# Two half-height matmul streams in the MLP of a small decoder trunk

## The chip, the cores and the metric

One core of one Trainium2 chip runs the whole program in one launch. The metric is device time in microseconds (us) of one execution. The engines have names that the profile uses: TensorE is PE (its weight loads are a row of their own, PEld), VectorE is DVE, ScalarE is ACT, GpSimd is POOL, SyncE is SP (it issues most DMAs). SBUF is the on-chip working memory of 128 partitions; PSUM is the accumulator memory that TensorE writes, eight banks of 512 fp32 values per partition.

## The reference, cut to what matters

A decoder trunk of two layers, 256 tokens, width 1024. Layer 0 has a mixer of convolution and pooling, layer 1 an attention mixer; each layer ends with a gated MLP of inner width 2816, and a final norm follows. The MLP is what the change touches:

```python
def conv_ffn(h, w_in, conv_w, conv_b, w_out):
    z = h @ w_in
    u, g = z[..., :D_FF], z[..., D_FF:]
    a = causal_dwconv(u, conv_w) + conv_b      # width 3 along the tokens
    return (jax.nn.silu(a) * g) @ w_out

h = h + conv_ffn(rmsnorm(h, ffn_norm_g[layer]), ...)
```

All values are fp32. The kernel keeps nearly that precision on TensorE by splitting each operand in two parts of a shorter format, hi and lo, and adding three products: hi by hi, hi by lo, lo by hi.

## The kernel before, in words

**Tiling.** Activations lie transposed, features on the 128 partitions and the 256 tokens along the row. The inner width of the MLP is cut into 22 chunks of 128 (index f). A step f computes the two input products of its chunk, u and g; each contracts 1024 features in eight chunks k of 128 rows. For each k, `in_halves` (lines 298 to 302) issues two matmuls. The first has the hi part of the weight as stationary operand and the hi and lo parts of the activation as one moving operand of 512 columns; it fills both halves of an accumulator bank. The second has the lo part of the weight and the hi part of the activation, 256 columns, and adds to the second half. That is 8 x 2 x 2 = 32 matmuls a step. The accumulators are `zu` and `zg`, one bank each, taken in turn from a pool of four banks, so that two steps are in flight.

**Behind the products.** `added` (line 527) adds the two halves of a bank: ScalarE copies one (line 532), VectorE adds the other (line 533). `gate` (line 536) scales by the norm's row, does the convolution (lines 388, 391, 392), SiLU (line 542) and the product with g (line 544), and splits the result y into hi and lo (lines 310 and 316).

**Output products.** y of chunk f is used LAG = 4 steps later. In layer 0 `Acc.add` (line 328) maps it to the eight chunks of 128 output features, three matmuls of 256 columns each (`mm3`, lines 276 to 279), 24 in all, on four accumulator banks `acc` that are kept through the layer. In layer 1 `TokenAcc.add` (line 350) has y as stationary operand and the weights as moving one, so that tokens end up on the partitions: four groups of three matmuls of 512 columns, 12 in all, on four banks `ta`, which first get the residual by 16 transposes (line 347).

**Order.** TensorE's order is that of the code (`manual_schedule(engines=ORDERED)`, line 54): u of step f, then g, then the output products of chunk f - 4, through the list `ffn_steps` (lines 66 to 71). After the last input step come the output products of chunks 18 and 19, and the last two chunks are closed chunk by chunk with what follows the MLP. The other engines' orders are made by a planner from the program and its own costs of each instruction.

**Weights.** They stream from HBM in blocks of 128 x 1024 fp32 (512 KB): u, g and output block of each step. SP loads a block into one of eight staging buffers (line 141), ScalarE makes the hi part (line 133), VectorE the lo part (line 134); hi and lo lie in a ring of seven pairs, and a pair is free again when the last matmul that reads it is done. Blocks are emitted in order of use, up to six ahead of the last one used (`ahead`, line 154).

**Elsewhere.** The attention's last product (`mix`, lines 745 to 752) writes the two heads of a pair to the two halves of the partitions of one bank; its stationary operand has 64 columns, so that each head uses one half of the array's columns. The norm's statistics use one-column matmuls (line 225). The MLP of layer 0 also writes a table for the attention to HBM by a DMA of POOL (line 595).

Of the kernel before, what the change touches and what calls it, by code (L numbers as in the profile page):

```python
# [18 lines left out]
P = 128  # L19
T = 256  # L20
D = 1024
NK = D // P
DFF = 2816
NF = DFF // P
# [9 lines left out]
LAG = 4  # L34
# [16 lines left out]
def trunk(ctx, tc, a, out):  # L51
    nc = tc.nc
# [83 lines left out]
    def emit_block(i):  # L136
        key, src = blocks[i]
        st, hi, lo = block_tiles(i)
        piece = 512 if i < 2 else BLK
        for s in range(0, BLK, piece):  # L140
            nc.sync.dma_start(st[:, s:s + piece], src[:, s:s + piece])
            cut(st, hi, lo, s, s + piece)
        done[key] = (hi, lo)
# [10 lines left out]
    def ahead(n=LOOK):  # L154
        while state["next"] < min(state["used"] + 1 + n, len(blocks)):
            emit_block(state["next"])
            state["next"] += 1

    def weights(key):
        state["used"] = max(state["used"], place[key])  # L160
        ahead(0)
        return done.pop(key)
# [18 lines left out]
    def col(i):  # L181
        return vec[:, i:i + 1]

    def new_hg():

        t = hgp.tile([P, NK, 2, T], F32R, tag="hg", name="hg")
        return t[:, :, 0, :], t[:, :, 1, :], t
# [12 lines left out]
    hg = new_hg()  # L200
# [46 lines left out]
    first = fst.tile([P, NK, FIRST], F32, name="first")  # L247
# [50 lines left out]
    def in_halves(z, w, k, x, first=False, last=False):  # L298

        wh, wl = (t[:, k * P:(k + 1) * P] for t in w)  # L300
        nc.tensor.matmul(z, wh, x[:, k], start=first, stop=False, skip_group_check=True)  # L301
        nc.tensor.matmul(z[:, 1, :], wl, x[:, k, 0, :], start=False, stop=last, skip_group_check=True)  # L302

    def split(pool_, src, scale, name, bufs=None, between=None):

        kw = {} if bufs is None else {"bufs": bufs}
        hi = pool_.tile([P, T], F32R, tag=name + "h", name=name + "h", **kw)
        lo = pool_.tile([P, T], F32R, tag=name + "l", name=name + "l", **kw)
        if scale is None:
            nc.scalar.copy(hi, src)  # L310
        else:
            nc.scalar.activation(hi, src, AF.Copy, scale=scale)
        if between is not None:
            between()
        if scale is None:
            nc.vector.tensor_sub(lo, src, hi.bitcast(F32))
        else:
            nc.vector.scalar_tensor_tensor(lo, src, scale, hi.bitcast(F32), op0=ALU.mult, op1=ALU.subtract)
        return hi, lo

    class Acc:
# [13 lines left out]
        def add_all(self, w, y):  # L335
            for dc in range(NK):
                self.add(dc, w, y, False)

    class TokenAcc:


# [13 lines left out]
        def add_all(self, w, y):  # L355
            for i in range(2):
                for n in range(2):
                    self.add(i, n, w, y, False)

    def close(acc, tail, b, between=None):  # L360

        for dc in (2 * b, 2 * b + 1):
            if dc % 2 and between is not None:
                between()
            for i, (w, y) in enumerate(tail):
                acc.add(dc, w, y, i == len(tail) - 1)
        c = slice(2 * b, 2 * b + 2)
        nc.vector.tensor_add(h[:, c, :], acc.t[b], resid["t"][:, c, :])

    def boundary(acc, tail, g0):  # L370

        st = Stats()
        hg = new_hg()
        with tc.high_priority(offset=PRIO):
            for b in range(4):
                close(acc, tail, b)
                scaled_h(hg, b, g0)
        for b in range(4):
            st.feed(b)
        ahead()  # L380
        return st, hg


    def conv_a(t, u, w0, bias=None):
        if bias is None:
            nc.scalar.activation(t, u, AF.Copy, scale=col(w0 + 2))
        else:
            nc.scalar.activation(t, u, AF.Identity, scale=col(w0 + 2), bias=bias)  # L388

    def conv_b(t, u, w0):  # L390
        nc.vector.scalar_tensor_tensor(t[:, 1:], u[:, :T - 1], col(w0 + 1), t[:, 1:], op0=ALU.mult, op1=ALU.add)
        nc.vector.scalar_tensor_tensor(t[:, 2:], u[:, :T - 2], col(w0), t[:, 2:], op0=ALU.mult, op1=ALU.add)
# [3 lines left out]
    with tc.tile_pool(name="ev", bufs=2) as ev, tc.tile_pool(name="evc", bufs=1) as evc:  # L396
# [27 lines left out]
        def pool_map(j):  # L424
            zp = psA.tile([P, 2, T], F32, tag="ps", name="zp")
            ph = pooled.pop(j)
            g = GROUPS[j]
            mm3(zp[:, 0, :], pwb[0][:, g * P:(g + 1) * P], pwb[1][:, g * P:(g + 1) * P], ph[0], ph[1], True, True)
            yb[j] = split(ev, zp[:, 0, :], col(V_PS + g), "yb", bufs=4)
# [34 lines left out]
        for k in range(NK):  # L464
# [3 lines left out]
            for n, (w, x, c) in enumerate(products):  # L468
                nc.tensor.matmul((zx0, zy0)[c // 2][:, c % 2, :], w[k // 2][:, k % 2, c * P:(c + 1) * P], hg[x][:, k, :],
                                 start=k == 0 and w is w0h and x == 0 and c % 2 == 0,  # L470
                                 stop=k == NK - 1 and w is w0l, skip_group_check=True)
# [22 lines left out]
        acc = Acc(psB)  # L494
# [17 lines left out]
        st, hg = boundary(acc, tail, V_FFN)  # L512
# [4 lines left out]
    def ffn(l, st, hg, ps_z, ps_acc, kind_acc, end, aside=None):  # L517
        with tc.tile_pool(name=f"ff{l}", bufs=2) as fp:
            acc = None
            ready = {}  # L520
            rrow = None
            z0 = None

            def new_z():
                return [ps_z.tile([P, 2, T], F32, tag="ps", name=f"z{c}") for c in "ug"]

            def added(z):

                zs = fp.tile([P, 2, T], F32, tag="zs", name="zs", bufs=3)
                zb = fp.tile([P, 2, T], F32, tag="zb", name="zb")  # L530
                for c in range(2):
                    nc.scalar.copy(zb[:, c, :], z[c][:, 1, :])
                    nc.vector.tensor_add(zs[:, c, :], z[c][:, 0, :], zb[:, c, :])  # L533
                return zs

            def gate(f, zs):
                nc.vector.tensor_mul(zs, zs, rrow[:, None, :].to_broadcast([P, 2, T]))  # L537
                t = fp.tile([P, T], F32, tag="t", name="t")
                conv_a(t, zs[:, 0, :], V_FC + (l * NF + f) * 3, bias=col(V_FB + l * NF + f))
                conv_b(t, zs[:, 0, :], V_FC + (l * NF + f) * 3)  # L540
                s = fp.tile([P, T], F32, tag="s", name="s")
                nc.scalar.activation(s, t, AF.Silu)
                y = fp.tile([P, T], F32, tag="y", name="y")
                nc.vector.tensor_mul(y, s, zs[:, 1, :])  # L544
                ready[f] = split(fp, y, None, "y_", bufs=LAG + 2)

            for kind, f in ffn_steps:
                if kind == "out":
                    if acc is None:
                        acc = kind_acc(ps_acc)  # L550
                    acc.add_all(weights(("fo", l, f)), ready.pop(f))
                    ahead()
                    continue
                wu, wg = weights(("fu", l, f)), weights(("fg", l, f))
                z = new_z()
                if f == 0:
                    for k in range(NK):
                        for c in range(2):
                            in_halves(z[c], (wu, wg)[c], k, hg[2], k == 0, k == NK - 1)
                    early = added(z)  # L560
                    ahead()
                    continue
                for c in range(2):
                    for k in range(NK):
                        in_halves(z[c], (wu, wg)[c], k, hg[2], k == 0, k == NK - 1)
                    if f == 1 and c == 0:
                        st.columns(ps_acc)
                    if f == 2 and c == 0:
                        rrow = st.rows()
                        for b in range(2):  # L570
                            gate(b, (early, zs)[b])
                zs = added(z)
                if f >= 2:
                    gate(f, zs)
                ahead()
                if aside is not None and f == 2:
                    aside(ps_acc)
            tail = [(weights(("fo", l, k)), ready.pop(k)) for k in (NF - 2, NF - 1)]
            return end(acc, tail)
# [4 lines left out]
    def t5_rows(ps):  # L584
# [10 lines left out]
        nc.gpsimd.dma_start(rowd, row[:, None, :].to_broadcast([NH, P, 384]))  # L595

    st, hg = ffn(0, st, hg, psA, psB, Acc, lambda acc, tail: boundary(acc, tail, V_MIX + NK), t5_rows)


    with tc.tile_pool(name="od", bufs=2) as od, tc.tile_pool(name="odc", bufs=1) as odc:  # L600
# [153 lines left out]
        ready = {}  # L754
# [41 lines left out]
        acc = Acc(psA)  # L796
# [16 lines left out]
        st, hg = boundary(acc, tail, V_FFN + NK)  # L813
# [31 lines left out]
    def ordered_final(acc, tail):  # L845
        with tc.manual_schedule(engines={mybir.EngineType.Activation, mybir.EngineType.DVE}):
            final(acc, tail)

    ffn(1, st, hg, psB, psA, TokenAcc, ordered_final)


# [72 lines left out]
```

## Time and profile before

| | us |
|---|---|
| median of 3 runs (lowest, highest) | 584.12 (583.64, 584.29) |
| the profiled execution, its own time | 583.38 |
| its span, first to last instruction | 581.6 |
| TensorE matmuls busy | 568.8 (98%) |
| TensorE weight loads busy | 512.4 (88%) |
| VectorE busy | 453.8 (78%) |
| ScalarE busy | 350.3 (60%) |
| POOL busy | 79.1 (14%) |

The profile is of one execution; the time outside its span is 1.8 us. A matmul's duration in it contains time in which the next one already runs, so the distance between the starts of two matmuls is what a matmul costs in a stream. The mean granted clock of TensorE is 0.994 of its full 2.4 GHz. Layer 0's MLP runs from about 78 to 270 us, layer 1's from 387 to 576 us.

### The profile page before, as it was taken

The numbers are of one execution on the slowest core, as the hardware profiler recorded it, in microseconds if no ns is written. First come the engines' busy times: TensorE is split into PE (matmuls) and PEld (weight loads), VectorE is DVE, ScalarE is ACT, GpSimd is POOL, SyncE is SP. The second block draws the span as 40 slices with busy tenths as digits, with TensorE's granted clock in tenths as the row PEclk, the third lists the DMA queues.
The fourth block names the chain that finished last, engine by engine and source line by source line (L and its number), as shares of the span: only waits on it lengthen the run. The fifth ranks groups of instructions, "written<-read, shape, count | busy, mean of one in ns | idle before, by whom it ended". The sixth has DMA issues, their size and how long they took to land.

```text
span 581.6 us, 9818 instructions
## 1 busy us (share of the span) xinstructions
PE 568.8 (98%) x3696; PEld 512.4 (88%) x3696; DVE 453.8 (78%) x784; ACT 350.3 (60%) x618; POOL 79.1 (14%) x91
## 2 busy tenths in 40 slices
PE   8999999998999999999999999999999999999995
PEld 7999998997999999999888999998888888888883
DVE  6999698944999777878688888578977787887752
ACT  7764476623667555557567776566755556555532
POOL 1531051000000000004171347031000000000000
PEclk9999999998999999999999999999999999999998
DMA  8966636578777655655656443447465555656001
GB/s 311 405 219 202 233 117 215 90 138 249 265 237 220 190 188 186 190 185 152 228 179 185 159 152 112 147 142 245 156 197 195 181 188 183 189 187 202 1 2 72
DMA packets 30896, 106.00 MB, mean 182 GB/s; under 512 B 4112, under 2 KB 4376, under 8 KB 30848
## 3 DMA queue, kind: packets, MB, share of 16 engines
q1 hardware_dynamic: 28944, 100.61, 52.8%
q0 software_dynamic: 1616, 4.24, 4.2%
q8 instruction: 29, 0.48, 0.3%
q10 hardware_dynamic: 288, 0.52, 0.2%
q14 instruction: 19, 0.16, 0.1%
HBM read 102.72 MB, written 2.63 MB: 181 GB/s over the span
## 4 chain that ended last, share of the span: by engine, by line
PE 71%; issue 9%; DMA 7%; DVE 6%; POOL 4%; ACT 1%; SPq 0%; POOLq 0%; ACTq 0%
PE zg L301 12%; PE zu L301 12%; PE zg L302 6%; PE zu L302 6%; DMA st<-in_ff_out 5%; PE acc L278 4%; PE acc L279 4%; PE acc L277 4%; PE ta L279 3%; PE ta L278 3%; PE ta L277 3%; DVE lo L134 2%; POOL nb L677 1%; PE pv L615 1%; PE pv L617 1%
## 5 line engine op out<-in xcount | busy, mean ns | idle before, releaser
L134 DVE TENSOR_TENSOR lo<-st,hi 128x1024 fp32r<-128x1024 f32 (+1 forms) x186 | 230.2, 1246 | 80.5 <-ACT hi L133 79.3
L133 ACT CAST hi<-st 128x1024 fp32r<-128x1024 f32 (+1 forms) x186 | 191.9, 1039 | 124.8 <-PE acc L278 22.0
L301 PE MATMUL zg<-hg,hi 128*128 128x512 f32 x352 | 127.9, 401 | 2.5 <-DVE zs L533 2.5
L301 PE MATMUL zu<-hg,hi 128*128 128x512 f32 x352 | 126.3, 397 | 0.3 <-DVE hg L197 0.3
L302 PE MATMUL zg<-hg,lo 128*128 128x256 f32 x352 | 99.3, 282 | 0.0
L302 PE MATMUL zu<-hg,lo 128*128 128x256 f32 x352 | 98.7, 280 | 0.0
L301 PEld LDWEIGHTS zg<-hg,hi 128*128 128x128 f32 x352 | 66.7, 190 | 18.5 <-DVE zs L533 2.8
L301 PEld LDWEIGHTS zu<-hg,hi 128*128 128x128 f32 x352 | 66.1, 188 | 15.9 <-DVE hg L197 0.6
L302 PEld LDWEIGHTS zu<-hg,lo 128*128 128x128 f32 x352 | 66.6, 189 | 0.8
L302 PEld LDWEIGHTS zg<-hg,lo 128*128 128x128 f32 x352 | 67.2, 191 | 0.0
L279 PE MATMUL acc<-y_h,lo 128*128 128x256 f32 x176 | 49.6, 282 | 0.0
L277 PE MATMUL acc<-y_h,hi 128*128 128x256 f32 x176 | 49.6, 282 | 0.0
L278 PE MATMUL acc<-y_l,hi 128*128 128x256 f32 x176 | 49.5, 281 | 0.0
L310 ACT CAST y_h<-y 128x256 fp32r<-128x256 f32 x44 | 17.8, 406 | 38.3 <-DVE y L544 38.3
L388 ACT ACTIVATE t<-zs,vec 128x256 f32<-128x256 f32 x44 | 26.4, 601 | 15.7 <-DVE zs L537 15.7
L217 POOL TENSOR_TENSOR sqs<-sq 128x512 f32<-128x512 f32 x4 | 5.2, 1294 | 223.9 <-ACT sq L212 223.9
L277 PE MATMUL ta<-hi,y_h 128*128 128x512 f32 x88 | 34.8, 395 | 0.0
L279 PE MATMUL ta<-hi,y_l 128*128 128x512 f32 x88 | 34.7, 395 | 0.0
L278 PE MATMUL ta<-lo,y_h 128*128 128x512 f32 x88 | 34.7, 395 | 0.0
L277 PEld LDWEIGHTS acc<-y_h,hi 128*128 128x128 f32 x176 | 33.1, 188 | 0.8
L279 PEld LDWEIGHTS acc<-y_h,lo 128*128 128x128 f32 x176 | 33.2, 188 | 0.0
L278 PEld LDWEIGHTS acc<-y_l,hi 128*128 128x128 f32 x176 | 33.1, 188 | 0.0
(222 smaller groups left out, 1211.3 us busy)
## 6 DMA issues: line engine op xcount, KB each, us to landing
st<-in_ff_in SPq DMA_DIRECT2D x88, 512.0 KB, 4.4
st<-in_ff_out SPq DMA_DIRECT2D x44, 512.0 KB, 4.3
st<-in_od_qk SPq DMA_DIRECT2D x16, 512.0 KB, 4.3
st<-in_ev_in SPq DMA_DIRECT2D x10, 512.0 KB, 7.1
st<-in_ev_out SPq DMA_DIRECT2D x8, 512.0 KB, 3.9
st<-in_od_v SPq DMA_DIRECT2D x8, 512.0 KB, 3.6
st<-in_od_out SPq DMA_DIRECT2D x8, 512.0 KB, 3.9
first<-in_first SPq DMA_DIRECT2D x7, 388.0 KB, 6.0
```

The costliest lines, as they stand in the source:

```text
L133: nc.scalar.copy(hi[:, s:e], st[:, s:e])
L134: nc.vector.tensor_sub(lo[:, s:e], st[:, s:e], hi.bitcast(F32)[:, s:e])
L277: nc.tensor.matmul(o, wh, xh, start=start, stop=False, skip_group_check=skip)
L278: nc.tensor.matmul(o, wh, xl, start=False, stop=False, skip_group_check=skip)
L279: nc.tensor.matmul(o, wl, xh, start=False, stop=stop, skip_group_check=skip)
L301: nc.tensor.matmul(z, wh, x[:, k], start=first, stop=False, skip_group_check=True)
L302: nc.tensor.matmul(z[:, 1, :], wl, x[:, k, 0, :], start=False, stop=last, skip_group_check=True)
L310: nc.scalar.copy(hi, src)
L388: nc.scalar.activation(t, u, AF.Identity, scale=col(w0 + 2), bias=bias)
L615: nc.tensor.matmul(pv[i], xh, wh, start=k == 0, stop=False)
L617: nc.tensor.matmul(pv[i], xl, wh, start=False, stop=k == NK - 1)
L677: nc.gpsimd.tensor_scalar(nb[:, T:], fbh[:, :P], fq[:, hh:hh + 1], None, op0=ALU.subtract)
```

## The change

Steps f = 4 to 21 of both MLPs are written anew. Each full matmul there (128 rows) becomes two of 64 rows: the upper 64 partitions of the weight and of the moving operand, and the lower 64. The two halves are issued one behind the other on two different accumulators. In a first turn (`in_rows`) the upper halves of u's products go to `zu` and the lower halves of g's products to `zg`; in a second turn the lists are swapped, and the lower halves of u's products go to `zu`, the upper halves of g's to `zg`. In the same way `add_rows` pairs two output accumulators, and half of an output step is the first turn of two pairs, the other half the second.

A step's order on TensorE is then: first turn of the input products, first half of the output products of chunk f - 4, second turn of the input products, second half of the output products. The first matmul of a turn that takes over banks waits until the last matmul of the turn before on these banks is done. That wait goes over POOL: a nop on POOL (`turn_ends`) waits for the matmul, and the next turn's first matmul waits for the nop. `added` and `gate` of a step come behind the second turn, and `ahead` once at the step's end. Steps 0 to 3 and the output products of chunks 18 to 21 stay as they were. In layer 1 the 16 transposes come ahead of step 4's input products instead of behind them.

```diff
@@ -301,6 +301,45 @@
         nc.tensor.matmul(z, wh, x[:, k], start=first, stop=False, skip_group_check=True)
         nc.tensor.matmul(z[:, 1, :], wl, x[:, k, 0, :], start=False, stop=last, skip_group_check=True)
 
+    ROWS = (slice(0, P // 2), slice(P // 2, P))
+    turns = {"last": None, "token": None}
+
+    def sync(ins, to):
+        tc.add_manual_dep(ins, to.name, mybir.DependencyInfo(mybir.DependencyClass.Sync, mybir.DependencyReason.DATA),
+                          reason="row halves take turns at a bank")
+
+    def row_mm(half, o, w, x, start, stop):
+
+        ins = nc.tensor.matmul(o, w[ROWS[half]], x[ROWS[half]], start=start, stop=stop, skip_group_check=True).ins
+        if turns["token"] is not None:
+            sync(ins, turns["token"])
+            turns["token"] = None
+        turns["last"] = ins
+
+    def turn_ends():
+
+        token = nc.gpsimd.nop().ins
+        sync(token, turns["last"])
+        return token
+
+    def in_rows(zs, ws, x, first, last):
+
+
+        for k in range(NK):
+            for lo in (0, 1):
+                for half, (z, w) in enumerate(zip(zs, ws)):
+                    wk = w[lo][:, k * P:(k + 1) * P]
+                    if lo:
+                        row_mm(half, z[:, 1, :], wk, x[:, k, 0, :], False, last and k == NK - 1)
+                    else:
+                        row_mm(half, z, wk, x[:, k], first and k == 0, False)
+
+    def mm3_rows(os, ss, ms, start):
+
+        for n, (i, j) in enumerate(((0, 0), (0, 1), (1, 0))):
+            for half in range(2):
+                row_mm(half, os[half], ss[half][i], ms[half][j], start[half] and n == 0, False)
+
     def split(pool_, src, scale, name, bufs=None, between=None):
 
         kw = {} if bufs is None else {"bufs": bufs}
@@ -336,6 +375,18 @@
             for dc in range(NK):
                 self.add(dc, w, y, False)
 
+        def add_rows(self, w, y, units):
+
+            for u in units:
+                bs = [(u + v) % 4 for v in (0, 2)]
+                for c in range(2):
+                    dcs = [2 * b + c for b in bs]
+                    mm3_rows([self.t[b][:, c, :] for b in bs],
+                             [[x[:, dc * P:(dc + 1) * P] for x in w] for dc in dcs], (y, y),
+                             [self.first[dc] and c == 0 for dc in dcs])
+                    for dc in dcs:
+                        self.first[dc] = False
+
     class TokenAcc:
 
 
@@ -356,6 +407,12 @@
             for i in range(2):
                 for n in range(2):
                     self.add(i, n, w, y, False)
+
+        def add_rows(self, w, y, units):
+            at = [divmod((u + v) % 4, 2) for u in units for v in (0, 2)]
+            for pair in zip(at[::2], at[1::2]):
+                mm3_rows([self.t[i][n] for i, n in pair], [[x[:, i * P:(i + 1) * P] for x in y] for i, n in pair],
+                         [[x[:, n * 512:(n + 1) * 512] for x in w] for i, n in pair], (False, False))
 
     def close(acc, tail, b, between=None):
 
@@ -544,15 +601,35 @@
                 nc.vector.tensor_mul(y, s, zs[:, 1, :])
                 ready[f] = split(fp, y, None, "y_", bufs=LAG + 2)
 
+            tokens = {}
+
+            def out_half(n, w, y):
+                turns["token"] = tokens.pop("out", None)
+                acc.add_rows(w, y, range(2 * n, 2 * n + 2))
+                tokens["out"] = turn_ends()
+
             for kind, f in ffn_steps:
                 if kind == "out":
-                    if acc is None:
-                        acc = kind_acc(ps_acc)
-                    acc.add_all(weights(("fo", l, f)), ready.pop(f))
-                    ahead()
+                    if f >= NF - LAG:
+                        acc.add_all(weights(("fo", l, f)), ready.pop(f))
+                        ahead()
                     continue
                 wu, wg = weights(("fu", l, f)), weights(("fg", l, f))
                 z = new_z()
+                if f >= LAG:
+
+                    if acc is None:
+                        acc = kind_acc(ps_acc)
+                    in_rows(z, (wu, wg), hg[2], True, False)
+                    token = turn_ends()
+                    w, y = weights(("fo", l, f - LAG)), ready.pop(f - LAG)
+                    out_half(0, w, y)
+                    turns["token"] = token
+                    in_rows(z[::-1], (wg, wu), hg[2], False, True)
+                    gate(f, added(z))
+                    out_half(1, w, y)
+                    ahead()
+                    continue
                 if f == 0:
                     for k in range(NK):
                         for c in range(2):
```

## Rows read from the trace of the kernel before

**Rows 1.** page, part 1: busy us (share of the span) xinstructions of each engine

```profile
PE 568.8 (98%) x3696; PEld 512.4 (88%) x3696; DVE 453.8 (78%) x784; ACT 350.3 (60%) x618; POOL 79.1 (14%) x91
```

**Rows 2.** busy by window, MLP steps: us, busy (x), clock, DMA, GB/s

```profile
182.26:250.26 68.00, 68.00 (x450) 62.06 (x449) 54.33 (x83) 39.53 (x64) 0.00 (x0) 1.00 0.61 194
470.76:554.59 83.83, 83.83 (x441) 71.59 (x440) 66.34 (x101) 49.10 (x80) 0.00 (x0) 1.00 0.47 152
```

**Rows 3.** timeline of PE, layer 0: start us, us, then the operation

```profile
191.00 0.28 PE L302 MATMUL zu<-hg,lo 128*128 128x256 f32 x1
191.12 0.40 PE L301 MATMUL zu<-hg,hi 128*128 128x512 f32 x1
```

**Rows 4.** timeline of weight loads (PEld), same place, same columns

```profile
191.00 0.19 PEld L301 LDWEIGHTS zu<-hg,hi 128*128 128x128 f32 x1
```

**Rows 5.** timeline of PE, value projection: first and last of 15 matmuls

```profile
270.16 0.39 PE L615 MATMUL pv<-hi,hg 128*128 128x512 f32 x1
...
273.33 0.39 PE L617 MATMUL pv<-hi,hg 128*128 128x512 f32 x1
```

**Rows 6.** PEld: four loads of the statistics, then the next load

```profile
23.07 0.54 PEld L225 LDWEIGHTS pst<-ones,tot 128*128 128x128 f32 x4
23.53 0.19 PEld L277 LDWEIGHTS zy<-hg,hi 128*128 128x128 f32 x1
```

**Rows 7.** timeline of PE, attention: a visit to 64-column tiles

```profile
332.04 0.28 PE L279 MATMUL zk<-hg,lo 128*128 128x256 f32 x1
332.25 0.66 PE L750 MATMUL po<-ptb,va 128*64 128x256 f32 x4
332.73 0.39 PE L751 MATMUL po<-ptb,va 128*64 128x128 f32 x4
333.05 0.39 PE L277 MATMUL zk<-hg,hi 128*128 128x256 f32 x1
333.28 0.28 PE L278 MATMUL zk<-hg,hi 128*128 128x256 f32 x1
```

**Rows 8.** timeline of PE, layer 1: twelve fp32 transposes, then a matmul

```profile
416.37 1.47 PE L347 MATMUL ta<-ident,h 128*128 128x128 f32 x12
417.60 0.48 PE L277 MATMUL ta<-hi,y_h 128*128 128x512 f32 x1
```

**Rows 9.** timeline of VectorE at the end: what POOL waited for

```profile
572.37 0.16 DVE L838 SCALAR_TENSOR_TENSOR var<-sums,var 128x1 f32<-128x1 f32 x1 [0.70 <-ACT junk L834]
```

**Rows 10.** POOL, whole span: first operation behind each MLP [idle before]

```profile
270.33 1.29 POOL L217 TENSOR_TENSOR sqs<-sq 128x512 f32<-128x512 f32 x1 [166.59 <-ACT sq L212]
...
572.60 0.55 POOL L839 TENSOR_TENSOR rcol<-var,mhalf 128x1 f32<-128x1 f32 x1 [172.92 <-DVE var L838]
```

**Rows 11.** VectorE and PE, layer 1: last y, first product reading it

```profile
565.11 0.43 DVE L316 TENSOR_TENSOR y_l<-y,y_h 128x256 fp32r<-128x256 f32 x1 [0.47 <-ACT y_h L310]
...
569.30 0.40 PE L277 MATMUL ta<-hi,y_h 128*128 128x512 f32 x1
```

**Rows 12.** VectorE and PE, layer 1: a block split, its first product

```profile
480.48 1.23 DVE L134 TENSOR_TENSOR lo<-st,hi 128x1024 fp32r<-128x1024 f32 x1 [0.63 <-ACT hi L133]
...
495.96 0.40 PE L301 MATMUL zu<-hg,hi 128*128 128x512 f32 x1
```

**Rows 13.** DMA, window 100:145: transfer, queue, count, KB each, us to landing

```profile
rowd<-row POOLq DMA_DIRECT2D x1, 1536.0 KB, 35.7
```

**Rows 14.** timelines and busy window, layer 0, around the pause

```profile
135.30 1.23 DVE L134 TENSOR_TENSOR lo<-st,hi 128x1024 fp32r<-128x1024 f32 x1 [4.27 <-ACT hi L133]
139.72 1.23 DVE L134 TENSOR_TENSOR lo<-st,hi 128x1024 fp32r<-128x1024 f32 x1 [3.20 <-ACT hi L133]
...
135.90 0.40 PE L301 MATMUL zu<-hg,hi 128*128 128x512 f32 x1
...
141.34 0.80 PE L301 MATMUL zg<-hg,hi 128*128 128x512 f32 x1 [2.46 <-DVE zs L533]
...
141.30:144.30 3.00, 2.96 (x9) 2.57 (x10) 2.94 (x5) 1.68 (x3) 0.00 (x0) 0.51 0.86 311
```

## The prediction

> **What bounds the kernel now.** Five views, in this order. The page's busy line first: TensorE's matmul row is busy for 98% of the span, VectorE for 78%, ScalarE for 60% [rows 1]. A busy share alone doesn't say whether the engine is at its own limit, so next the busy times by stretch, taken over whole MLP steps: 8 steps of layer 0 last 68.00 us and 10 steps of layer 1 last 83.83 us, and in both PE is busy for all of it, at a granted clock of 1.00, its level of 2.4 GHz [rows 2]. That is 8.50 us a step in layer 0 and 8.38 us in layer 1, with no pause: the matmul stream itself is the bound. The reader is to see that nothing but a cheaper stream, or a pause somewhere else, can move these 36 steps (f = 4 to 21 of both layers, some 304 us of the span).
>
> Third, the timeline of one step: a 256-column matmul starts 0.12 us before the next one, and the weight load of the matmul after it starts in the same hundredth as the matmul before it [rows 3, 4]. So each load already runs under a matmul. Fourth, two stretches that price the stream from outside the MLP. In the value projection, 512-column matmuls with full loads follow each other at 3.17/14 = 0.226 us, 0.113 per 256 columns [rows 5]. Four loads with one-column matmuls take 0.46 us, 0.115 each [rows 6]: a load by itself needs as long as 256 columns. Fifth, the only place in which tiles of the array already work side by side: the attention's last product, below.
>
> **The change part by part.** Count a step in units of 256 columns: the input products are 16 matmuls of 512 and 16 of 256, 48 units; the output products are 24 of 256 in layer 0 or 12 of 512 in layer 1, 24 units. Together 72. The change keeps the columns, halves the rows of each matmul and doubles the matmuls and the loads: 112 of each for 56 in layer 0, 88 for 44 in layer 1. What decides is the price of a pair of halves against one full matmul; the trace of before has no 64-row matmul, so I bound it.
>
> *Below.* A pair moves the same columns, and the best that any fp32r stretch shows is 0.113 per unit [rows 5]: 72 x 0.113 = 8.15 us a step, 0.35 less than layer 0 has and 0.23 less than layer 1. 18 x (0.35 + 0.23) = 10.4 us gained.
>
> *Above.* If loads of the two halves can't overlap, a step takes 112 x 0.115 = 12.9 us in layer 0 and 88 x 0.115 = 10.1 in layer 1: 18 x (4.4 + 1.7) = 110 us lost.
>
> *The nearest row.* The attention's product writes two heads into two 64-column tiles; the code issues all matmuls of one head ahead of the other's. Four passes of 256 columns last from 332.25 to 332.73, 0.48 us [rows 7]. One stream would need 4 x 0.205 = 0.82: passes of the same type (plain fp32) on the full array take 1.23/12 = 0.1025 per 128 columns [rows 8]. So two tiles ran side by side, with their loads, and neither waited for the other's earlier place in the order. These are column tiles, not row tiles, but they are the row nearest to it, and they say that a pair costs about one. I take the pair at today's price: 0 us for the 36 steps.
>
> The Trainium skill would have it otherwise: TensorE: Matmul & The Clock Gate, Part 3, says that a weight load overlaps matmuls in flight only when its row group differs. By that rule the full-row loads of before would stand exposed and the change would hide them; the trace disagrees, since full-row loads start with the matmul before them [rows 3, 4] and 256 columns with a load take 0.118 where columns alone take 0.113. By the rule as it stands more than half of a step would come back; by the rows at most the 10.4 us above.
>
> *Changing the tile size.* The visit to column tiles lasts from 332.16 (the end of the full matmul's 0.12) to 333.16 (333.28 less 0.12) [rows 7]: 1.00 us, of which two streams in parallel explain 2 x 0.205 + 2 x 0.1025 = 0.615. The other 0.385 is the way in and out. The change has one such visit a layer (steps 4 to 21; the last output products stay full): 2 x 0.385 = +0.77 us.
>
> *The tokens.* Each step adds three nops on POOL that wait for a turn's last matmul, and two waits on PE. What is queued behind a waiting matmul is all of PE's later work, and everything waits for that. The cover is the other turn: 12 to 24 pairs, 1.4 us at least. POOL answers VectorE in 0.07 us (572.53 to 572.60) [rows 9], and from step 4 on it has nothing else to do in either MLP: it is idle for 166.6 us before the first sum behind layer 0 and for 172.9 us before the end [rows 10]. Cost 0; without the cover, and with a nop as long as POOL's 0.55 us operation, 72 waits would cost 40 to 50 us.
>
> *What moves.* Both accumulators of a step end 7.1 us into it instead of at a third and two thirds, so of the 14.2 us (two steps of 8.5 less the third that u's products take, 2.8) until a bank is needed again, VectorE and ScalarE lose 4.3; the gate branch moves 1.4 us. y of a step is read four steps later, and at the end y(21) is ready at 565.54 where the last products read it at 569.30 [rows 11]: 3.8 us less 1.4, still early. The weight blocks: u and g of a step are held until 7.1 us into it (two turns of 2.8 and the output half of 1.4 between them), not 2.8 and 5.7, and g and the output block are wanted 2.8 us earlier. Today a block is split at 480.48 + 1.23 = 481.71 and used at 495.96, 14.2 us later [rows 12]; at most 4.3 + 2.8 of that go. Cost 0, hidden by the ring's depth. Loads on SP keep their order, and VectorE's work stays 54.33/8 = 6.8 us a step of 8.5 [rows 2].
>
> *The one pause.* In layer 0 a 1.5 MB table write holds the DMA engines for 35.7 us [rows 13]. Splits of step 8's blocks come late, ScalarE's copy of an older accumulator stands behind them, and PE waits 2.46 us at 141.34; then it runs at a clock of 0.51, the 1.2 GHz level, for some 3 us [rows 14], about 4 us in all. With the change, step 8 (start 135.90) wants g at once and has it at 136.53; the output block, wanted 2.8 us on, comes at 140.95: 0.6 + 1.6 = 2.2 us of waits. Net -0.3; bounds -4 (no pause, no slow clock) and +4.
>
> *Sum.* Against the profiled execution's 583.38 us (span 581.6 and 1.8 around it): 0 + 0.77 - 0.3 = 583.9. The median of the runs lies 0.74 higher, so 584.6.
>
> **The rivals.**
> (1) *The load's share goes away.* Matmuls today cost 0.118 where 0.113 is possible [rows 2, 5]; if the excess belongs to the load of the same rows, and a half's load costs its stream less, up to 10.4 us come back: 574.2. For: the value projection shows that it is not fixed. Against: it has full-row loads too, so rows aren't what sets it.
> (2) *The halves lean on each other.* Twice the loads, each with today's excess for both streams: 10.4 us lost, 595. The tile visit's pair, 0.24 against 0.205, would say 0.035 x (56 + 44) x 18 = 63 us, but this has the way in with it.
> (3) *Loads one after the other* (the side of slower): in the input products, the load of the second half waits for the first half's; it decides once two loads (0.23) take longer than the pair's matmul, so in all of the 256-column pairs. +110: 694. Against it stand the column tiles, whose loads overlapped. The change would not do what it says here; matmuls of the halves one after the other too would be 304 us more.
> (4) *A wait in each step:* accumulators or split blocks late, because VectorE's order, written for other due times, stands behind a late matmul. 0.5 us a step is +18: 602. For: 80% of VectorE is taken. Against: the 9.9 and 7.1 us that are left.
>
> **How the numbers follow.** Pair at today's price 0.47 (own range 581 to 589, by the pause's bounds); rival 1 0.28; 2 0.13; 3 0.07; 4 0.05. Less than 0.2% (1.2 us) can't be told from no change here. Faster: 0.28 + 0.12 from the forecast's lower side = 0.40; same: 0.21; slower: 0.14 + 0.13 + 0.07 + 0.05 = 0.39. The range goes from 570 (rival 1 with the pause gone) to 606 (rival 4, and rival 2 with the pause grown); rival 3, the far side of 2 and anything cheaper than rows 5 show are left out, some 0.17.
>
> **What would show it.** Starts of the two halves of a pair within some hundredths of each other, and pairs 0.117 to 0.119 per unit apart; under 0.116 is rival 1, 0.12 to 0.125 rival 2, 0.23 for 256-column pairs with 0.115 between all starts is rival 3. Busy times of a step of 8.4 to 8.5 us with no wait of PE for POOL. A PE idle row with zs or lo as releaser in every step is rival 4. The forecast is wrong if the step's length moves by more than 0.1 us either way.

## The result, and the profile after

The changed kernel takes 588.42 us (median of 6 runs, 586.03 to 589.34), the kernel before beside it 583.88 (583.58 to 584.59): a ratio of 1.0071, interval 1.0051 to 1.009. It is 4.5 us slower. The forecast was 584.6 with a range of 570 to 606; the time lies in the range, but no measurable change was forecast and the kernel is slower. The profiled execution is the fastest of the six: 586.03 us against 583.38 of the profile before, +2.65. The two do not have the same clock: before, a stretch at 0.51 stands behind the pause [rows 14]; in the new profile the granted clock is 1.00 from 100 to 576 us. Against the 20 later executions of the kernel before with a mean clock of 0.996 to 0.998 (median 582.25 us; the 28 with 0.994 or 0.995: 583.8), and so at about the clock of the new profile (0.996), the loss is 3.8 us.

The busy line of the page, for [rows 1]: twice as many matmuls as the code had in these steps, and hardly more busy time (569.7 against 568.8).

```profile
PE 569.7 (98%) x5496; PEld 522.2 (89%) x5496; DVE 451.5 (77%) x784; ACT 349.1 (60%) x618; POOL 79.4 (14%) x91
```

Next, for [rows 2], whole steps: 7 steps of layer 0 from the start of step 14 and 16 steps of layer 1. The columns are the stretch, its length, busy times of the five engines with their instructions, granted clock, DMA share and GB/s.

```profile
189.79:248.92 59.13, 59.13 (x790) 59.13 (x787) 47.50 (x74) 34.66 (x58) 0.00 (x0) 1.00 0.65 199
426.73:561.13 134.40, 134.40 (x1411) 114.36 (x1408) 103.85 (x161) 78.56 (x128) 0.00 (x0) 1.00 0.53 165
```

59.13/7 = 8.447 us a step where it was 8.50, and 134.40/16 = 8.400 where it was 8.38. So the loss is not in the steps. The start of the first row turn, for [rows 3, 4], shows the two halves of a pair starting in the same hundredth, and a pair of 512 and a pair of 256 columns together taking 0.35, 0.117 per unit:

```profile
102.12 0.28 PE L313 MATMUL zu<-hg,lo 64*128 64x256 f32 x1
102.12 0.28 PE L313 MATMUL zg<-hg,lo 64*128 64x256 f32 x1
102.24 0.39 PE L313 MATMUL zu<-hg,hi 64*128 64x512 f32 x1
102.24 0.39 PE L313 MATMUL zg<-hg,hi 64*128 64x512 f32 x1
102.47 0.27 PE L313 MATMUL zu<-hg,lo 64*128 64x256 f32 x1
102.47 0.27 PE L313 MATMUL zg<-hg,lo 64*128 64x256 f32 x1
```

What is new stands in the view of waits (engine, tile, line, releaser: us in total, times, longest). Before, TensorE had one MLP wait, 2.46 us [rows 14]. Now there are four, and the longest is at the end of layer 0, for the last y. The other three stand in step 7 (131.45 us; "issue" means that the profile shows nothing that TensorE waited for), in step 8 (140.74) and at the start of step 9 (147.34):

```profile
PE acc L277 <- ACT y_h L349: 2.3, 1, 2.3
PE zu L313 <- DVE zs L590: 0.9, 1, 0.9
PE acc L313 <- issue: 0.8, 1, 0.8
PE acc L313 <- DVE lo L134: 0.5, 1, 0.5
```

**Where the 2.65 us come from.** The two traces are cut at the same matmuls. Up to step 4: -0.20. From step 4 to the output products of chunk 18 in layer 0: 101.78 to 257.68 against 101.98 to 258.76, -0.88, where the kernel before has its stretch at half clock and the new one has none. From there to the value projection: 257.68 to 272.12 against 258.76 to 270.16, +3.04. To step 4 of layer 1: -0.16. From step 4 to chunk 18 there (412.18 to 565.42 against 410.38 to 563.02): +0.6. The rest: +0.25. One stretch, the end of layer 0, holds the whole loss.

**Why y is late there.** Step 21's accumulators end at 256.05 + 0.28 = 256.33, but ScalarE copies them only at 258.57. The starts of that copy (`zb<-zu`) in steps 5 to 8, 20 and 21:

```profile
118.94 0.36 ACT L589 COPY zb<-zu 128x256 f32<-128x256 f32 x1
134.87 0.36 ACT L589 COPY zb<-zu 128x256 f32<-128x256 f32 x1
145.60 0.36 ACT L589 COPY zb<-zu 128x256 f32<-128x256 f32 x1
153.67 0.36 ACT L589 COPY zb<-zu 128x256 f32<-128x256 f32 x1
250.49 0.37 ACT L589 COPY zb<-zu 128x256 f32<-128x256 f32 x1
258.57 0.36 ACT L589 COPY zb<-zu 128x256 f32<-128x256 f32 x1
```

The copies of steps 5 and 6 lie 15.93 us apart, for a step of 8.45. The table write of [rows 13] is why: ScalarE waits for weight blocks from HBM, 6.29 us in the row below, with VectorE and the rest of the chain from z to y behind it. By step 7 the copy is 10.1 us behind its accumulator. From then on it comes every (258.57 - 153.67)/13 = 8.07 us, so it makes good 0.38 us a step against TensorE's 8.45, and 13 steps give back 4.9. In layer 1, where no table is written, the copy follows the accumulators at 0.87 us in every step from 4 to 20.

```profile
126.82 1.05 ACT L133 CAST hi<-st 128x1024 fp32r<-128x1024 f32 x1 [6.29 <-DMA st<-in_ff_in]
```

The end of the layer, VectorE's rows of the last y, with the fourth split of this step right ahead of it, and TensorE's rows around it:

```profile
264.28 1.22 DVE L134 TENSOR_TENSOR lo<-st,hi 128x1024 fp32r<-128x1024 f32 x1
265.42 0.42 DVE L601 TENSOR_TENSOR y<-s,zs 128x256 f32<-128x256 f32 x1
266.31 0.42 DVE L355 TENSOR_TENSOR y_l<-y,y_h 128x256 fp32r<-128x256 f32 x1 [0.47 <-ACT y_h L349]
```

```profile
263.78 0.28 PE L279 MATMUL acc<-y_h,lo 128*128 128x256 f32 x1
266.33 0.39 PE L277 MATMUL acc<-y_h,hi 128*128 128x256 f32 x1 [2.27 <-ACT y_h L349]
```

And the same place before: y(21) done at 262.39, its first reader at 264.82, 2.4 us to spare.

```profile
261.96 0.43 DVE L316 TENSOR_TENSOR y_l<-y,y_h 128x256 fp32r<-128x256 f32 x1 [0.47 <-ACT y_h L310]
```

```profile
264.82 0.28 PE L277 MATMUL acc<-y_h,hi 128*128 128x256 f32 x1
```

Before, the copies fell behind as far (14.1 us for u of step 7) but were on time again by step 14: there the planner had woven the chain of one step into the next, and VectorE was busy for 45.14 of the 49.35 us between the copies of u in steps 7 and 14. With both accumulators ending together and late, the planner makes one closed chain per step, in which VectorE waits for ScalarE three times (0.55, 0.47 and 0.52 us) and no other work stands in the gap.

### The profile page after: what moved, and what is told of

The parts are those of the page before. It is cut to its first block, busy times and chain, and to the rows that moved or that the text cites. A ratio compares the mean times of both kernels' runs of the same rounds, so it can differ in the third digit from the quotient of the medians.

```text
span 584.3 us, 13555 instructions
## 1 busy us (share of the span) xinstructions
PE 569.7 (98%) x5496; PEld 522.2 (89%) x5496; DVE 451.5 (77%) x784; ACT 349.1 (60%) x618; POOL 79.4 (14%) x91
## 4 chain that ended last, share of the span: by engine, by line
PE 65%; issue 11%; DVE 8%; DMA 8%; POOL 4%; ACT 3%; SPq 0%; POOLq 0%; ACTq 0%; DVEq 0%
PE zu L313 15%; PE zg L313 14%; PE ta L313 9%; PE acc L313 6%; DMA st<-in_ff_out 5%; DVE lo L134 3%; PE zu L301 2%; PE zg L301 2%; PE acc L278 2%; PE acc L279 1%; PE acc L277 1%; POOL nb L754 1%; PE pv L692 1%; PE pv L694 1%; PE pv L693 1%
## 5 line engine op out<-in xcount | busy, mean ns | idle before, releaser
L313 PE MATMUL zu<-hg,hi 64*128 64x512 f32 x576 | 204.8, 392 | 0.9 <-DVE zs L590 0.9
L313 PE MATMUL zg<-hg,hi 64*128 64x512 f32 x576 | 205.7, 394 | 0.0
L313 PE MATMUL zu<-hg,lo 64*128 64x256 f32 x576 | 159.8, 277 | 0.0
L313 PE MATMUL zg<-hg,lo 64*128 64x256 f32 x576 | 159.6, 277 | 0.0
L313 PEld LDWEIGHTS zu<-hg,hi 64*128 64x128 f32 x576 | 106.2, 184 | 9.3 <-DVE zs L590 1.1
L313 PEld LDWEIGHTS zg<-hg,hi 64*128 64x128 f32 x576 | 106.4, 185 | 8.2
L313 PEld LDWEIGHTS zu<-hg,lo 64*128 64x128 f32 x576 | 106.9, 186 | 0.7
L313 PEld LDWEIGHTS zg<-hg,lo 64*128 64x128 f32 x576 | 106.7, 185 | 0.8
L313 PE MATMUL acc<-y_l,hi 64*128 64x256 f32 x288 | 53.9, 280 | 0.8 <-issue 0.8
L313 PE MATMUL acc<-y_h,lo 64*128 64x256 f32 x288 | 53.8, 281 | 0.5 <-DVE lo L134 0.5
```

Of the source, the lines that this page charges most:

```text
L313: ins = nc.tensor.matmul(o, w[ROWS[half]], x[ROWS[half]], start=start, stop=stop, skip_group_check=True).ins
```

## The experiments

Theory A: the halves cost and give nothing; the loss is the backlog of the table write, which the changed order of a step pays off too slowly. Theory B: the halves themselves cost. Each kernel was timed beside the kernel before.

**e1: the changed kernel, the table written in eight pieces.** One piece a step, behind TensorE's first turn of steps 4 to 11:

```diff
-        nc.gpsimd.dma_start(rowd, row[:, None, :].to_broadcast([NH, P, 384]))
+        def piece(i, behind):
+            ins = nc.gpsimd.dma_start(rowd[i:i + 1], row[i:i + 1, None, :].to_broadcast([1, P, 384])).ins
+            tc.add_manual_dep(ins, behind.name, ...)   # not before this matmul
...
+                    if aside is not None and f < LAG + NH:
+                        piece(f - LAG, turns["last"])
```

> Theory A (backlog): the loss is not in the row halves but in VectorE's and ScalarE's chain from z to y. The 1.5 MB table write holds up the weight blocks of steps 5 to 8 of layer 0; the chain falls 10.5 us behind, and because in the changed order of the step it needs 8.07 us a step against TensorE's 8.45, it makes good only 0.38 us a step and is still 2.2 us late at step 21, so that the last output products wait 2.3 us. Here the table is written in eight pieces, one in each of steps 4 to 11. A expects: no wait of TensorE over 0.3 us between 100 and 270 us (2.1 in three waits in steps 6 to 9 and 2.3 at the end of layer 0 are gone), z to y_l within 9 us in all steps from 4 on, and 586.0 - 4.4 = 581.6 us, median within 1 us of that. Rival B (the halves themselves: skew of the two streams at each turn, tokens, twice the instructions): the table has little to do with it, 585 to 589 us as before.

Measured: 582.05 us (581.31 to 584.25, 12 runs), ratio 0.9986 (0.9973 to 0.9999). Writing the table in pieces, with nothing else changed, takes 6.4 us off the changed kernel. The waits of steps 7 to 9 are gone. A part of A missed: z to y_l grew from 9.1 us in step 4 to 12.5 in step 12 and shrank after it by 0.38 a step, and a wait stayed at the end of the layer. In steps 5 to 12 the planner's order had put one split more ahead of the copies, and the chain took 8.83 us a step. So the chain can fall behind without the table.

```profile
PE acc L277 <- ACT y_h L351: 1.4, 1, 1.4
```

**e2: the kernel before, table in eight pieces.** The same edit in the old order.

> The kernel before, with the same table in eight pieces in steps 4 to 11. Theory A: its one pause (2.46 us at 141 us) and the slow clock behind it go, 4 us: 579.9 us, so that the row halves without any backlog cost 581.6 / 579.9 = 1.003. Rival B: also about 580 here, but with e1 at 585 to 589 the ratio would stay at or above 1.009.

Measured: 588.15 us (587.87 to 589.54, 5 runs), ratio 1.0094 (1.0077 to 1.0112). A miss for A. The pause is gone and y(21) is ready at 258.18, 4.2 us sooner than before, but a new wait of 6.3 us stands at the next place: the norm's sum at the end of layer 0. In the new order ScalarE's squares come behind splits that wait for the value projection's matmuls; the second of four stands at 275.32 where before it was done by 270.24. Behind the wait the granted clock is 0.50 from 282 to 286 us.

```profile
274.36 1.05 ACT L133 CAST hi<-st 128x1024 fp32r<-128x1024 f32 x1 [1.71 <-PE pv L625]
275.32 0.62 ACT L212 ACTIVATE sq<-h 128x512 f32<-128x512 f32 x1
```

**e3: the changed order with full matmuls.** No halves, no tokens; each input product's row blocks 0 to 3 in the first part of a step and 4 to 7 in the second:

```diff
-                    in_rows(z, (wu, wg), hg[2], True, False)
+                    for k in range(NK // 2):
+                        for c in range(2):
+                            in_halves(z[c], (wu, wg)[c], k, hg[2], k == 0, False)
...
-                acc.add_rows(w, y, range(2 * n, 2 * n + 2))
+                acc.add_half(n, w, y)   # two banks in full
```

> The changed order of a step (half of the input products, half of the output products, the other halves; both accumulators end together late in the step), but with full 128-row matmuls, no halves side by side and no tokens. VectorE and ScalarE get the same order of instructions as in the changed kernel. Theory A: the same backlog and the same wait at the end of layer 0 (about 2 us), 585 to 588 us. Rival B: without the halves the loss goes, 583 to 584.5 us.

Measured: 589.29 us (589.2 to 589.67, 4 runs), ratio 1.0109 (1.0089 to 1.013), above A's range and at least as slow as the halves. B falls: without a single half the same waits are there, the last one longer. The steps are 8.447 and 8.400 us, as with the halves.

```profile
PE acc L277 <- ACT y_h L349: 4.0, 1, 4.0
PE zu L301 <- DVE zs L598: 1.9, 2, 1.0
```

Here the wait at the end of the layer is followed by a granted clock of 0.5, the 1.2 GHz level, for 6.8 us:

```profile
266.00:270.00 4.00, 2.23 (x9) 2.06 (x10) 1.71 (x3) 0.73 (x2) 0.00 (x0) 0.60 0.84 230
270.00:274.00 4.00, 4.00 (x22) 4.00 (x22) 2.26 (x4) 1.79 (x4) 0.00 (x0) 0.55 0.39 152
```

**e4: the changed kernel, the chain's order by hand.** In steps 4 to 21 ScalarE and VectorE follow the code, and the three splits of a step stand in the chain's gaps:

```diff
-                    gate(f, added(z))
                     out_half(1, w, y)
-                    ahead()
+                    with tc.manual_schedule(engines={mybir.EngineType.Activation, mybir.EngineType.DVE}):
+                        gate_and_split(f, added(z))   # hi, scale, conv, lo, hi, conv, SiLU, lo, hi, y, y_h, lo, y_l
+                        ahead()
```

> The changed kernel with row halves and the table in one write, but in steps 4 to 21 the order of VectorE and ScalarE is written out by hand: the three splits of a step stand in the gaps of the chain from z to y (a split while ScalarE starts the convolution, one during SiLU, one during the cast of y), so VectorE needs its busy 6.4 us a step and no idle time. Theory A: the chain makes good 1.5 to 2 us a step, is on time by step 15, and the wait of 2.3 us at the end of layer 0 goes; the waits in steps 6 to 9 stay: 583 to 585.5 us. Rival B: nothing changes for TensorE, 585 to 589 us.

Measured: 582.83 us (582.41 to 587.58, 12 runs), ratio 1.001 (0.9993 to 1.0028). Nearly as A says, 0.2 us under its range: z to y_l is 14.8 us in step 7, then 7.5 in step 8 and 7.05 from step 9 on (A had step 15); the long wait at the end of the layer is gone but for 0.4 us. The waits behind the table stay. The profiled execution took 585.66 us, and its granted clock is 0.50 from 144 to 146 us, behind these waits.

```profile
PE acc L313 <- ACT hi L600: 1.4, 1, 1.4
PE acc L313 <- DVE lo L607: 0.8, 1, 0.8
PE zg L313 <- DVE lo L607: 0.7, 1, 0.7
PE acc L278 <- DVE y_l L355: 0.4, 1, 0.4
```

**e5: e2 with the table's source row in its own tile.**

```diff
-        row = nrm.tile([P, 2, T], F32, tag="sq", name="row")
+        row = nrm.tile([NH, 384], F32, tag="row", name="row", bufs=1)
```

> The kernel before with the table in eight pieces, as in e2, but the table's source row in a tile of its own. In e2 the row sat in one of the two tiles of the squared sums until its last piece, the order of ScalarE at the end of layer 0 put three of the four squares behind five splits, and TensorE waited 6.3 us for POOL's sum at 282 us. Theory A: with the old order of the squares that wait is gone and so is the pause of layer 0: 588.15 - 6.3 - about 2 of slow clock behind it = 579.9 us. Rival: the order at the end of layer 0 comes out late again, 583 us or more.

Measured: 587.89 us (586.88 to 588.61, 6 runs), ratio 1.0075 (1.0059 to 1.0091). The rival was right: the shared tile was not the reason, and two of the four squares are late again.

```profile
281.55 1.02 PE L225 MATMUL pst<-ones,tot 128*128 128x1 f32 x4 [5.59 <-POOL tot L222]
```

**e6 and e7: halves against full matmuls, nothing else in the way.** Both have the table in pieces, the chain of e4, and at the end of layer 0 an order by hand with each block's squares right behind its scaling (in step 21 the third split follows y). e6 has the halves, e7 the full matmuls of e3.

> Row halves, table in eight pieces (source row in its own tile), VectorE's and ScalarE's order in steps 4 to 21 and at the end of layer 0 written by hand. Theory A: no wait of TensorE from 100 to 265 us, z to y_l 7.1 us in every step; against e1 (582.05) the wait of 1.4 us at the end of layer 0 goes: 580.3 us, within 0.5 us of e5 (e5 has steps of 8.50 and 8.38 us and no visits to another tile size; here 18 x 8.447 + 18 x 8.40 and 2 x 0.4 us of visits). Rival B (halves cost by themselves): 2 us or more above e5 and e7.

> As e6 in everything, but full 128-row matmuls in the same places (each input product's first four row blocks in the first part of a step, the last four in the second; each output half as full matmuls) and no tokens. Theory A: steps of 8.45 and 8.40 us as with the halves, since e3 showed the same; only the two visits to another tile size are saved: 0.8 us below e6, 579.5 us. Rival B: 2 us or more below e6. Rival C (halves hide something): above e6.

Measured: e6 581.85 us (581.44 to 583.37, 12 runs), ratio 0.9978 (0.9967 to 0.999); e7 580.53 us (580.23 to 581.42, 6 runs), ratio 0.9953 (0.9937 to 0.9969). The halves are 1.3 us dearer: more than A's 0.8, less than B's 2, and both kernels are over A's times (580.3 and 579.5). Seven steps of layer 0 and 13 of layer 1, first of e6, then of e7:

```profile
186.46:245.59 59.13, 59.13 (x789) 54.27 (x786) 45.45 (x71) 34.35 (x57) 0.00 (x0) 1.00 0.58 187
426.44:535.64 109.20, 109.20 (x1147) 93.02 (x1144) 84.44 (x131) 63.87 (x105) 0.00 (x0) 1.00 0.59 188
```

```profile
187.31:246.44 59.13, 59.13 (x395) 54.26 (x394) 45.57 (x71) 34.87 (x57) 0.00 (x0) 1.00 0.57 187
426.63:535.83 109.20, 109.20 (x573) 93.01 (x572) 84.69 (x131) 64.76 (x105) 0.00 (x0) 1.00 0.57 189
```

789 matmuls and 395 take the same 59.13 us. The difference of 1.3 us is outside the steps: two visits to the other tile size (e8) are 0.83 of it; e6's wait for the norm's row at the end of layer 0 is 0.5 us longer than e7's in the traces (1.1 against 0.6), and no run shows why. The two profiled executions themselves took the same time (581.44 and 581.42 us): in parts where the kernels are alike e7's lost 1.3 us, 1.0 of it ahead of the table's product in layer 0 and 0.3 between the last norm's sums and step 4 of layer 1. So the terms are read stretch by stretch: 0.38 in the MLP of layer 0, 0.53 around the norm's row, 0.41 in the MLP of layer 1.

**e8: only the input products in halves.** As e6 with e3's full output products, so that the tile size changes four times a step.

> As e6, but only the input products in row halves, the output products as full matmuls, so that TensorE changes the tile size four times a step instead of twice a layer. The prediction's price of a visit (way in and out) was 0.385 us from the column tiles; the entry at 101.8 us and the exit at 257.7 us of the changed kernel show about 0.2 us each. 36 steps x 2 visits x 0.4 = 28.8, less the 0.8 of e6: 580.3 + 28 = 608 us, steps of 9.25 and 9.2 us. If the change of size costs nothing by itself: 580.

Measured: 610.97 us (610.86 to 611.37, 4 runs), ratio 1.0473 (1.0454 to 1.0492): 29.1 us over e6 for 72 visits in place of 2, 0.416 each. The way out of the halves and the way back, around 12 full matmuls:

```profile
202.38 0.28 PE L315 MATMUL zg<-hg,lo 64*128 64x256 f32 x1
202.59 0.39 PE L277 MATMUL acc<-y_h,hi 128*128 128x256 f32 x1
202.81 0.28 PE L278 MATMUL acc<-y_l,hi 128*128 128x256 f32 x1
202.93 0.28 PE L279 MATMUL acc<-y_h,lo 128*128 128x256 f32 x1
...
204.00 0.28 PE L279 MATMUL acc<-y_h,lo 128*128 128x256 f32 x1
204.21 0.50 PE L315 MATMUL zu<-hg,hi 64*128 64x512 f32 x1
204.55 0.28 PE L315 MATMUL zu<-hg,lo 64*128 64x256 f32 x1
```

From 202.38 to 202.59 and on to 202.81 are 0.43 us for two units of 0.117; from 204.00 to 204.55 are 0.55 for three. About 0.2 us each way. The Trainium skill, TensorEngine Tiling (Array Packing), Tiling Modes, says that a change of the tiling mode drains the engine. The trace fits this, with 0.42 us for the two changes of a visit.

**e9: the kernel before, pieces, end of layer 0 by hand.** Old order of a step, no halves.

> The kernel before (old order of a step, no halves) with the table in eight pieces and, so that the late squares of e2 and e5 can't come back, with VectorE's and ScalarE's order at the end of layer 0 written by hand (each block's squares right behind its scaling), as in e6 and e7. Theory A: the pause of 2.46 us with its slow clock in layer 0 and the 5.6 us wait at the end of layer 0 are both gone: e5's 587.9 - 5.6 - 2 = 580.3 us, so level with e7 (580.5, full matmuls in the changed order) and 1 to 1.5 us below e6 (581.85, halves). Rival: the pause of the kernel before cost less than 4 us, 582 us or more, and the changed order has a gain of its own.

Measured: 580.32 us (579.89 to 580.61, 5 runs), ratio 0.995 (0.9936 to 0.9964). As A says. TensorE waits nowhere in the MLP, and the kernel is level with e7. These two are the fastest versions found, 3 us under the kernel before; neither has the halves.

**e10: the changed kernel once more.**

> The changed kernel itself, one more profile. Its profile had 586.0 us and a mean clock of 0.996, the fastest of its runs; the others had 587.6 to 589.3 at 0.991 to 0.995. Theory A: a run of about 588.5 has the same waits (some 2 us in steps 6 to 9, 2.3 at the end of layer 0) and behind one of them a stretch of some 4 us at half clock. Rival: the missing 2.4 us lie in longer steps.

Measured: a single run of 586.09 us at a clock of 0.996 with the waits of the first profile (2.3 at the end of layer 0, 2.1 in steps 8 and 9). It is no run of 588.5, so it doesn't tell where the other 2.4 us go. Half clock behind one of the waits, as in the traces of e3 and e4, would lower the mean clock as four of those runs have it (0.991 to 0.993); the slowest, 589.34 us, has 0.995 and doesn't fit. No trace of the changed kernel itself shows half clock in its MLPs, so this stays open.

## Why the prediction was right and where it was wrong

**The main term, 0 us for the pairs: right, almost to the hundredth.** A step of halves is as long as a step of full matmuls in the same order, 59.13 us for seven (e6, e7). The bounds, -10.4 and +110, were far too wide; the column tiles were the right row to lean on. Of the signs named, starts within some hundredths hold only where the streams begin together (102.12); later one stream leads by up to some 0.3 us. The 8.447 for 8.50 in layer 0 and 8.40 for 8.38 in layer 1 belong to the order of the matmuls, since e3 and e7 have them without halves: 18 x (-0.053 + 0.017) = -0.6 us. Rivals 1, 2 and 3 (load's share, halves leaning on each other, loads one after the other) are out. So is the rule of the Trainium skill as the prediction took it (TensorE: Matmul & The Clock Gate, Part 3, loads overlap only where the row group differs; the same Part also lets a load into the background weight buffer go ahead). By that rule e7 would have its 128-row loads exposed and be far slower than e6; it is 1.3 us faster.

**The tile size, +0.77: right.** e8 gives 0.416 a visit, 0.83 for two, taken from column tiles and found again with row tiles.

**The tokens, 0: right.** The code has three waits a step, not two, from the second step on. But no matmul of the steps waits for POOL in any trace, and e6's steps with tokens equal e7's without. The cover named, the other turn, is there.

**The pause, -0.3 with bounds -4 and +4: right in size, in part by luck.** The three waits of steps 7 to 9 and what they disturb cost 155.90 (step 4 to chunk 18) - 18 x 8.447 - 0.42 = 3.4 us, where the pause of before cost 156.78 - 18 x 8.50 = 3.8 by the same sum. The waits are 2.1 us, for 2.2 forecast, but at other places; the forecast had the slow clock behind them again, and the profile doesn't have it. What makes up the other 1.3 us is not taken apart. e1 and e9 show that the table write is behind both.

**What moves, "Cost 0, hidden by the ring's depth": this step failed.** It said of the end that "y(21) is ready at 565.54 where the last products read it at 569.30 [rows 11]: 3.8 us less 1.4, still early". Two things were wrong with it. The row was layer 1's, where no table is written and no splits follow; layer 0 had 2.4 us to spare, not 3.8, though 2.4 less 1.4 would still have been early. And the chain from z to y was taken to keep its length and move as a whole by 1.4 us. It was written anew by the planner: 6.3 us from z to y_l at the end of layer 0 before, 10.4 after, because it was still 2.2 us late from the table write 120 us earlier and had four splits ahead of y where the chain of before had two. The price is +3.0 us, 2.3 of it the wait for y, and it is the loss. Rival 4 had the mechanism (VectorE's order, written for other due times) but put it in every step at 0.5 us; the steps don't see it, only the end of the layer does, where y has no four steps of slack left. For the same reason the sign named for a wrong forecast, a step longer or shorter by over 0.1 us, never came, though the kernel got slower.

The forecast's sum, 583.9 for a profiled execution, with the failed term (+3.0) and the order's -0.6 gives 586.3; 586.03 was measured. The further 2.4 us of the median over that profile were not foreseen: the median of before lay 0.74 above its profile. That the time lies in the range is in part luck: the upper end, 606, was there for rival 4 in every step and for rival 2 with a longer pause, and neither came.

## What to carry to other kernels

Halving the rows of a matmul stream whose loads already run under the matmuls bought nothing here: two half streams took to the hundredth what one full stream took, and each change of tile size cost about 0.2 us. When a step's order changes, look at the chain behind it at the end of the loop and in every layer, not where the slack is largest, and ask how fast that chain makes good a delay, not only whether it keeps up. Where a planner writes an engine's order, any edit can move a stall to a place far from it (e2, e5): compare the whole order, and write by hand the few places that TensorE waits for.

## What the runs showed of the hardware

The two row tiles don't keep to the program's order between them. Below, the output products of the upper half start at 192.57 and 192.69, ahead of the lower half's last input matmul at 192.71, which stands earlier in the code; one stream can lead the other by some 0.3 us, and neither loses by it.

```profile
192.57 0.28 PE L313 MATMUL acc<-y_h,hi 64*128 64x256 f32 x1
192.69 0.28 PE L313 MATMUL acc<-y_l,hi 64*128 64x256 f32 x1
192.71 0.28 PE L313 MATMUL zg<-hg,lo 64*128 64x256 f32 x1
```

The order of the same 56 full matmuls has a small price of its own in layer 0: with u and g by turns and the output products in two halves the step takes 8.447 us (e7), with u first, then g, then all output products 8.50 (e9). Which of the two differences does it is not shown. And a DMA of 1.5 MB that TensorE never waits for itself was worth 3 to 6 us by the loads it held up: 6.4 in e1 and 3.3 in e9, there with the end of layer 0 ordered by hand. In e2 and e5, without that order, the planner took more than this back.
